# A two-layer trunk in split fp32 on one core: another deal of the first chunk's taps, six products moved behind the convolution's output, and two weights whose low parts VectorE subtracts

## The chip, the cores and the metric

The kernel runs on one core of one Trainium2 chip. The metric is device time in microseconds (us) of one execution. The kernel before was timed three times: 1772.48, 1773.45 and 1774.38 us, median 1773.45 us. Its profiled execution took 1771.89 us by the same clock, of which the trace covers a span of 1770.1 us; so the profiled execution is 1.56 us faster than the median, and 1.79 us of it lie outside the span.

The engines are called as in the profile: PE is TensorE's matmul, PEld its weight load, DVE is VectorE, ACT is ScalarE, POOL is GpSimd, SP is SyncE, which here only issues DMAs.

## What is computed

Two residual layers over a sequence of 1024 positions with 1024 channels, one sequence, everything in fp32. Each sub-layer is an RMS norm, a shift and scale from a conditioning vector, the sub-layer, a gate and the residual sum. Layer 0 mixes tokens with a convolution module, layer 1 with a pooling mixer; both have a gated feed-forward part of width 2816.

```python
def conformer_conv(h, w1, b1, w_dw, b_dw, ln_g, ln_b, w2, b2):
    u = h @ w1 + b1
    a, g = jnp.split(u, 2, axis=-1)
    u = a * jax.nn.sigmoid(g)
    u = depthwise_causal_conv(u, w_dw) + b_dw        # width 31
    u = jax.nn.silu(layer_norm(u, ln_g, ln_b))       # over channels
    return u @ w2 + b2

for i in range(2):
    sh_m, sc_m, g_m, sh_f, sc_f, g_f = split(silu(c) @ ada_w[i] + ada_b[i])
    h = modulate(rms_norm(x, norm_mix_g[i]), sh_m, sc_m)
    y = conformer_conv(h, ...) if i == 0 else multiscale_pool(h, ...)
    x = x + (1 + g_m) * y
    h = modulate(rms_norm(x, norm_ffn_g[i]), sh_f, sc_f)
    x = x + (1 + g_f) * ((silu(h @ w_gate[i]) * (h @ w_up[i])) @ w_down[i])
return rms_norm(x, final_g)
```

## The kernel before

**Tiles.** Channels lie on the 128 partitions, in 8 tiles (KT = 8); the sequence is cut into two chunks of 512 positions, A and B. Every fp32 operand of a product is kept as a high part and a low part. A weight tile of 128 x 1024 so becomes a pair of `w` tiles, and for each of its 8 pieces k PE makes three products of 512 columns (`products`): high weight by high activation, high weight by low activation, low weight by high activation. Twenty-four products make one output tile.

**Lows of weights.** `load_weight` brings the raw weight with an SP DMA, ACT casts it to the high part, and the low part is raw minus high. In most cases it is made without DVE: ACT writes minus the high part into the low tile, and POOL issues a DMA that adds the raw weight on top of it from memory (line 461, seen in the profile as `POOL L461 DMA w<-in_...`). Weights that are wrapped in `Own` are instead subtracted by DVE (`w<-raw,w`). There are nine `w` buffers and four `raw` buffers.

**The depthwise convolution.** 31 taps for each of 8 channel tiles and each chunk. For tile 7 of chunk A, PE does it. For the others, `Taps.step` deals each tap to DVE or to POOL. On DVE a tap is one instruction (`ca<-u,taps,ca`). On POOL it is two: ACT scales the row (`ny<-u,taps` in chunk A, `pr<-u,taps` in chunk B) and POOL adds it to a running sum (`pa<-pa,ny` or `pa<-pa,pr`). At the end DVE adds POOL's sum to its own (`ca<-pa,ca`) and puts the last tap in place (`u<-u,taps,ca`).

**What sets the order.** PE's instructions run in the order in which the code emits them, written out by hand. The other engines' order is made from the same program by a scheduler that respects dependences. Which engine gets a tap or a part of a side task is decided while the program is written out, by estimated clocks: `clock["PE"]` moves with every product, `clock["V"]` (DVE) and `clock["G"]` (POOL) with every instruction by the prices in `PRICES`, and `pace` hands out work to whichever engine's clock is not more than `AHEAD` in front of PE's. A `Task` is a chain that says at each stop how long it must be left alone; the stops are looked up in `LOAD`. The stop "mean" stands in `layer_norm_silu` for chunk A between the last sum of channels (`acc<-acc,u`) and PE's `mean` product; the larger the number, the later on PE's clock the mean is written out.

**The stretch that matters.** In order of PE: products `a` and `g` of chunk B with A's taps running on DVE and POOL beside them; the layer norm of A (`mean`, then `var`, then `rstd`) placed among those products; then the last pair of B, emitted by `conv_split`: all of its `a`, then the first `EARLY_K` pieces of its `g`, the rest being held back (`st["split"]`). Then `y`, the second matrix of the convolution for A, 8 output tiles. Then the first feed-forward norm of A. `norm_split` puts the held products of `g` around its two steps on PE: `COVER_K` says up to which piece k they go ahead of `var` and ahead of `rstd`, the rest follows `rstd`; `COVER` says how many idle products (`idle<-ones`, results thrown away) are added at each of the three places. With the norm's results (`hhi`, `hlo`) the feed-forward part of A starts: `ffn_first` runs gate and up of f = 0 and gate of f = 1 together, then up of f = 1; `ffn_p1` runs gate and up of the following f; after every two f the group `dn` multiplies by the down weights. In this stretch DVE and POOL do B's taps. `fa` is the list of these units; its first three are replaced by `ffn_first` and the unit of f = 2 with its weights wrapped in `Own`. The fourth is the first `dn` group, which needs `dn` weights of f = 0 and 1.

**Names in the profile.** Every DVE, ACT and POOL computation has the line 119 (`Engine.issue`), every product the line 142; so instructions are told apart by the tiles they write and read.

Of the kernel before, what the change touches and what calls it, by code (L numbers as in the profile page):

```python
# [45 lines left out]
PHTAPS = 29  # L46
PHLEN = 135
OUT_B = 3
LOAD = {"load": 9.0, "late": 5.0, "second": 11.0, "settle": 8.0, "mean": 11.0, "slow": 18.0, "next": 4.0}
AHEAD = 4  # L50
STRETCH = 1.35
LATER = 300
WARM = (22, 10, 6)
COVER, EARLY_K, COVER_K = (2, 2, 4), 3, (5, 8)
FREE = 4
EARLY_X = 4
WARM_LAST = 5
# [67 lines left out]
def trunk(ctx, tc, xT, c, vec, ada, adan, w1, w2, wgu, wdn, wpl, wph, out):  # L125
# [488 lines left out]
    def own(unit_):  # L614
        return unit_[0], tuple(Own(w) for w in unit_[1])
# [109 lines left out]
    class Taps:  # L725
# [10 lines left out]
        def step(self, e):  # L736
            ch, p = self.ch, self.p
            n = ch.n
            u = st["u", ch.i, p]
            w = lambda j: wdw[:, j * KT + p : j * KT + p + 1]  # L740
            if self.done:
                return False
            if self.next < CW - 1:
                if e == "V" and self.acc is None and sum(isinstance(t, Taps) and t.acc is not None for t in tasks) >= 2:
                    return False
                if e == "G":
                    if self.acc is None and self.part is None and sum(isinstance(t, Taps) and t.part is not None for t in tasks) >= 2:
                        return False
                    if self.next >= CW - 3:
                        return False  # L750
                j = self.next
                self.next += 1
                if e == "V":
                    src = u[:, j : j + n]
                    if self.acc is None:
                        self.acc = spare_bank("ca")
                        V_.tensor_scalar(self.acc, src, w(j), V("conv_bdw", p), op0=MUL, op1=ADD)
                    else:
                        V_.scalar_tensor_tensor(self.acc, src, w(j), self.acc, op0=MUL, op1=ADD)
                    st["tap"] = V_.last.ins.name  # L760
                    twin = [t for t in tasks if isinstance(t, Taps)][:2]
                    if len(twin) == 2 and twin[0] is self:
                        i, k = (tasks.index(t) for t in twin)
                        tasks[i], tasks[k] = tasks[k], tasks[i]
                elif self.part is None:
                    self.part = window(n, "pa")
                    G_.tensor_scalar(self.part, u[:, j : j + n], w(j), 0.0, op0=MUL, op1=ADD)
                    if st.get("behind norm"):
                        tc.add_manual_dep(G_.last.ins, st.pop("behind norm"), synced, reason="behind the norm")
                else:  # L770
                    pr = temp(n, "ny", 2) if ch.i == 0 else temp(n, "pr")
                    S_.activation(pr, u[:, j : j + n], AF.Copy, scale=w(j))
                    scaled_taps.append(S_.last.ins)
                    G_.tensor_tensor(self.part, self.part, pr, op=ADD)
                return True
            if e != "V":
                return False
            if self.part is not None:
                V_.tensor_tensor(self.acc, self.part, self.acc, op=ADD)
            d = u[:, HALO : HALO + n]  # L780
            V_.scalar_tensor_tensor(d, d, w(CW - 1), self.acc, op0=MUL, op1=ADD)
            self.done = True
            tasks.remove(self)
            left = st["taps", ch.i]
            left[p] = True
            return True
# [271 lines left out]
    def ffn_first(ch, l, between):  # L1058

        def emit(take):  # L1060
            h = st["h", ch.i]
            outs = [output(name, False) for name in ("gate", "up", "gate")]
            wts = [take() for _ in outs]
            for k in range(KT):
                for o, wt in zip(outs, wts):
                    products(o, wt, k, h[k], k == 0, k == KT - 1)
                pace()
                if k == 3:
                    between()
                if k == FREE:  # L1070
                    del scaled_taps[:]
            gated(ch, 0, outs[:2], held=scaled_taps)
            hold[0] = st["silu"]
            wt = take()
            outs.append(output("up", False))
            for k in range(KT):
                products(outs[3], wt, k, h[k], k == 0, k == KT - 1)
                if k % 4 == 3:
                    pace()
                    if k == 3:  # L1080
                        del scaled_taps[:]
            gated(ch, 1, outs[2:], held=scaled_taps)
        return emit, tuple(wgu[l, f, i] for f in range(2) for i in range(2))
# [980 lines left out]
    taps(B, *range(KT))  # L2064
    put("ln_b", lambda: layer_norm_silu(B))
    fa = ffn(A, 0, False)
    fa[:GROUP + 1] = [ffn_first(A, 0, gates_on), own(fa[GROUP])]
    for i, (e, ws) in enumerate(fa):
        if i == len(fa) - OUT_B:
            need("ln_b")  # L2070
# [182 lines left out]
```

## Time and profile before

| what | value |
|---|---|
| median of three timed runs | 1773.45 us |
| profiled execution, own time | 1771.89 us |
| span of its trace | 1770.1 us |
| PE busy in the span | 1738.5 us |
| DVE busy | 1374.0 us |
| ACT busy | 987.1 us |
| POOL busy | 564.0 us |

A line of the timeline gives the start in us, the time that the instructions took, engine, line, operation, output and inputs by the program's names, shapes and how many were merged; in brackets stands the idle time of the engine just before it and who ended it. A line of the chain of work gives start, duration, engine, name and the number of instructions. A line of a table of windows gives the stretch, its length, then for PE, PEld, DVE, ACT and POOL the busy time with the number of instructions, then the granted PE clock as a share of full speed, the DMA share and GB/s. A line of the DMA view ends with the size of one transfer and the median time from its issue to its landing. Waits are listed as "who waited, for what: us in total, times, longest".

### The profile page before, as it was taken

The page shows a single profiled execution, that of the slowest core. Times are in us where ns is not written, and L with a number is a line of the kernel's source. Part 1 is how long each engine was busy: PE and PEld are TensorE (multiplying, and loading weights), DVE is VectorE, ACT ScalarE, POOL GpSimd, SP SyncE. Part 2 cuts the span into 40 slices and gives each one's busy share as a digit, 9 for nine tenths or more (in the row PEclk, how much of TensorE's full clock was granted, in tenths as well). Part 3 has the DMA queues.
Part 4 walks back from the last instruction along what each step waited for, and adds up shares of the span by engine and source line. Part 5 has one row for each costly group of instructions (what it writes and reads, how often), then busy time and mean ns, then how long its engine had stood idle before and what let it go on. Part 6 is the DMA issues. An engine that isn't in the chain of part 4 may idle for free.

```text
span 1770.1 us, 24916 instructions
## 1 busy us (share of the span) xinstructions
PE 1738.5 (98%) x8830; PEld 1460.3 (82%) x8830; DVE 1374.0 (78%) x2273; ACT 987.1 (56%) x1566; POOL 564.0 (32%) x607
## 2 busy tenths in 40 slices
PE   9999999999999999999999999999999999999997
PEld 7777787788888888899999888887888888877996
DVE  7999657788775327989996977976888788777885
ACT  4776656767656455555555356464444444444653
POOL 0599614887834121211102713411011111111112
PEclk9999999999999999999999999999999999999999
DMA  9959746988988988877675477798778888887551
GB/s 296 305 171 251 196 118 157 243 214 213 240 204 205 240 218 195 222 210 215 198 213 132 123 179 177 166 235 272 226 216 262 240 242 223 252 251 201 155 150 54
DMA packets 145151, 366.26 MB, mean 207 GB/s; under 512 B 14977, under 2 KB 32641, under 8 KB 145026
## 3 DMA queue, kind: packets, MB, share of 16 engines
q1 hardware_dynamic: 109600, 265.56, 44.5%
q0 software_dynamic: 34272, 98.06, 31.3%
q8 instruction: 69, 1.13, 0.3%
q10 hardware_dynamic: 1154, 1.05, 0.2%
q14 instruction: 56, 0.46, 0.1%
HBM read 340.50 MB, written 24.12 MB: 206 GB/s over the span
## 4 chain that ended last, share of the span: by engine, by line
PE 89%; DMA 4%; issue 2%; DVE 2%; ACT 1%; POOL 1%; SPq 0%; DVEq 0%; POOLq 0%; ACTq 0%
PE gate L142 24%; PE dn L142 24%; PE up L142 23%; PE y L142 6%; PE a L142 3%; PE g L142 3%; PE first L142 2%; DMA adaw<-in_adan_dram 1%; DMA t<-t 1%; DMA w<-in_wdn_dram 1%; PE ada L142 1%; DMA front<-front 1%; DVE x L119 1%; ACT w L119 0%; DMA w<-in_wgu_dram 0%
## 5 line engine op out<-in xcount | busy, mean ns | idle before, releaser
L119 ACT CAST w<-raw 128x1024 fp32r<-128x1024 f32 (+1 forms) x314 | 262.7, 838 | 110.6 <-PE up L142 46.1
L142 PE MATMUL dn<-ghi,w 128*128 128x512 f32 (+1 forms) x944 | 302.6, 386 | 2.7 <-DMA w<-in_wdn_dram 2.1
L142 PE MATMUL gate<-hhi,w 128*128 128x512 f32 (+1 forms) x968 | 295.1, 373 | 1.3 <-ACT hhi L119 0.8
L142 PE MATMUL up<-hhi,w 128*128 128x512 f32 (+1 forms) x968 | 294.6, 372 | 0.0
L119 ACT ACTIVATE w<-raw 128x1024 fp32r<-128x1024 f32 (+1 forms) x182 | 172.9, 950 | 193.1 <-PE up L142 60.0
L119 DVE SCALAR_TENSOR_TENSOR x<-dn,gains,x 128x512 f32<-128x512 f32 (+1 forms) x312 | 225.5, 733 | 46.9 <-PE dn L142 45.2
L142 PEld LDWEIGHTS gate<-hhi,w 128*128 128x128 f32 x968 | 178.1, 189 | 34.6 <-ACT hhi L119 1.0
L142 PEld LDWEIGHTS dn<-ghi,w 128*128 128x128 f32 x944 | 176.3, 189 | 36.6 <-DMA w<-in_wdn_dram 2.5
L142 PEld LDWEIGHTS up<-hhi,w 128*128 128x128 f32 x968 | 178.0, 188 | 31.8
L142 PE MATMUL dn<-glo,w 128*128 128x512 f32 (+1 forms) x472 | 181.9, 385 | 0.1
L142 PE MATMUL gate<-hlo,w 128*128 128x512 f32 (+1 forms) x484 | 180.2, 372 | 0.3 <-DVE hlo L119 0.3
L142 PE MATMUL up<-hlo,w 128*128 128x512 f32 (+1 forms) x484 | 179.8, 372 | 0.0
L119 DVE SCALAR_TENSOR_TENSOR ca<-u,taps,ca 128x512 f32<-128x512 f32 x251 | 174.9, 747 | 0.9
L461 POOL DMA_DIRECT2D w<-in_wgu_dram x76 | 69.0, 907 | 247.3 <-ACT w L119 233.2
L1547 POOL DMA_DIRECT2D x<-scaled x48 | 41.6, 868 | 325.9 <-ACT scaled L119 170.2
L119 DVE TENSOR_TENSOR w<-raw,w 128x512 fp32r<-128x512 f32 (+1 forms) x132 | 108.9, 831 | 41.8 <-ACT w L119 34.9
L119 POOL TENSOR_TENSOR pa<-pa,pr 128x512 f32<-128x512 f32 x92 | 131.5, 1509 | 8.4 <-ACT pr L119 6.4
L119 DVE TENSOR_TENSOR t<-t,up 128x512 f32<-128x512 f32 (+1 forms) x76 | 49.4, 650 | 89.7 <-PE up L142 87.1
L1215 POOL DMA_DIRECT2D w<-in_wgu_dram x42 | 37.1, 891 | 256.3 <-ACT w L119 109.5
L119 POOL TENSOR_TENSOR pa<-pa,ny 128x512 f32<-128x512 f32 x77 | 104.0, 1381 | 8.5 <-ACT ny L119 5.8
L142 PEld LDWEIGHTS gate<-hlo,w 128*128 128x128 f32 x484 | 91.3, 189 | 16.6 <-DVE hlo L119 0.6
L142 PEld LDWEIGHTS up<-hlo,w 128*128 128x128 f32 x484 | 91.1, 188 | 15.9
(292 smaller groups left out, 3844.4 us busy)
## 6 DMA issues: line engine op xcount, KB each, us to landing
raw<-in_wgu_dram SPq DMA_DIRECT2D x148, 512.0 KB, 5.6
t<-t SPq DMA_DIRECT2D x224, 256.0 KB, 5.2
w<-in_wgu_dram POOLq DMA_DIRECT2D x76, 512.0 KB, 8.2
adaw<-in_ada_dram SPq DMA_DIRECT2D x64, 512.0 KB, 5.1
raw<-in_wdn_dram SPq DMA_DIRECT2D x62, 512.0 KB, 5.5
raw<-in_w_dram SPq DMA_DIRECT2D x42, 512.0 KB, 6.2
w<-in_wdn_dram POOLq DMA_DIRECT2D x34, 512.0 KB, 8.3
adaw<-in_adan_dram SPq DMA_DIRECT2D x32, 512.0 KB, 5.7
```

The costliest lines, as they stand in the source:

```text
L119: self.last = self.order(getattr(self.eng, name)(out, *args, **kw))
L142: last_mm[0] = nc.tensor.matmul(out, lhsT, rhs, start=start, stop=stop, **kw).ins.name
L461: order(nc.gpsimd.dma_start(as_src(lo), src, accum_op=ADD))
L1215: order(nc.gpsimd.dma_start(lo, src, accum_op=ADD))
L1547: order(nc.gpsimd.dma_start(st["kept", "x"][at], t, accum_op=ADD))
```

## The change

Three edits, in four places of the text.

First, chunk A's taps: each POOL sum of chunk A now moves POOL's estimated clock by a further 0.08, and the stop "mean" is 7 in place of 11. Second, the products held for the norm: `EARLY_K` is 1 in place of 3, so 3 products of the last `g` and not 9 stand ahead of `y`; `COVER_K` (4, 7) puts 9 ahead of `var`, 9 ahead of `rstd` and 3 behind it, in place of 6, 9 and none; the idle products of the three places are 0, 0 and 2 in place of 2, 2 and 4. Third, the down weights of f = 0 and f = 1 are wrapped in `Own`, so DVE subtracts their lows.

```diff
-LOAD = {"load": 9.0, "late": 5.0, "second": 11.0, "settle": 8.0, "mean": 11.0, "slow": 18.0, "next": 4.0}
+LOAD = {"load": 9.0, "late": 5.0, "second": 11.0, "settle": 8.0, "mean": 7.0, "slow": 18.0, "next": 4.0}
 AHEAD = 4
+SLOWER = 0.08
...
-COVER, EARLY_K, COVER_K = (2, 2, 4), 3, (5, 8)
+COVER, EARLY_K, COVER_K = (0, 0, 2), 1, (4, 7)
...
                     S_.activation(pr, u[:, j : j + n], AF.Copy, scale=w(j))
                     scaled_taps.append(S_.last.ins)
                     G_.tensor_tensor(self.part, self.part, pr, op=ADD)
+                    if ch.i == 0:
+                        clock["G"] += SLOWER
...
-    fa[:GROUP + 1] = [ffn_first(A, 0, gates_on), own(fa[GROUP])]
+    fa[:GROUP + 2] = [ffn_first(A, 0, gates_on), own(fa[GROUP]), own(fa[GROUP + 1])]
```

Where this moves instructions is shown at three places; a number in a name is that of one tile, and the numbers differ between the two programs for the same tile.

POOL, ahead of chunk A's mean: `pa` is POOL's running sum of the last channel tile, `ny` a row that ACT scaled, `DMA w` the issue of a weight's low, and `u<-u,ny` is the first work behind the mean. Before:

```order
L461 DMA w_1966<-in_w_dram 128x1024
L119 TENSOR_TENSOR pa_1728<-pa_1728,ny_1849 128x512
L119 TENSOR_TENSOR pa_1728<-pa_1728,ny_1881 128x512
L119 TENSOR_TENSOR pa_1728<-pa_1728,ny_1885 128x512
L119 TENSOR_TENSOR pa_1728<-pa_1728,ny_1889 128x512
L461 DMA w_2086<-in_w_dram 128x1024
L119 TENSOR_TENSOR pa_1728<-pa_1728,ny_1907 128x512
L119 TENSOR_TENSOR pa_1728<-pa_1728,ny_1911 128x512
L461 DMA w_2097<-in_w_dram 128x1024
L119 TENSOR_TENSOR u_653<-u_653,ny_2037 128x512
```

With the change:

```order
L462 DMA w_1957<-in_w_dram 128x1024
L120 TENSOR_TENSOR pa_1756<-pa_1756,ny_1914 128x512
L120 TENSOR_TENSOR pa_1756<-pa_1756,ny_1918 128x512
L462 DMA w_2080<-in_w_dram 128x1024
L462 DMA w_2091<-in_w_dram 128x1024
L120 TENSOR_TENSOR u_653<-u_653,ny_2031 128x512
```

Two sums in place of six stand behind the same weight's DMA, and none behind the next one. Over the whole of chunk A POOL has 74 sums in place of 77, DVE 129 taps in place of 126; for chunk B POOL has 96 in place of 92 and DVE 136 in place of 140. The `mean` product stands at the same place of PE's order as before.

PE, from the end of `y` to the first gate product: `g` are the held products, `idle` the idle ones. Before:

```order
L142 MATMUL ada_2522<-adaw_2533,ccols 32x256 x4
...
L142 MATMUL g_2184<-hhi_767,w_2097 128x512
L142 MATMUL idle_2646<-ones 128x128 x2
L142 MATMUL var_2627<-ones,acc_2368 128x1 x4
L142 MATMUL g_2184<-hhi_769,w_2096 128x512
...
L142 MATMUL g_2184<-hhi_773,w_2097 128x512
L142 MATMUL idle_2662<-ones 128x128 x2
L142 MATMUL rstd_2678<-ident,col_2666 128x128 x4
L142 MATMUL idle_2683<-ones 128x128 x4
L142 MATMUL gate_2738<-hhi_2611,w_2517 128x512
```

With the change:

```order
L143 MATMUL ada_2510<-adaw_2521,ccols 32x256 x4
...
L143 MATMUL g_2178<-hhi_765,w_2091 128x512
L143 MATMUL var_2615<-ones,acc_2356 128x1 x4
L143 MATMUL g_2178<-hhi_767,w_2090 128x512
...
L143 MATMUL g_2178<-hhi_771,w_2091 128x512
L143 MATMUL rstd_2663<-ident,col_2651 128x128 x4
L143 MATMUL g_2178<-hhi_773,w_2090 128x512
L143 MATMUL g_2178<-hlo_774,w_2090 128x512
L143 MATMUL g_2178<-hhi_773,w_2091 128x512
L143 MATMUL idle_2671<-ones 128x128 x2
L143 MATMUL gate_2724<-hhi_2599,w_2505 128x512
```

The last piece of `g` now stands behind `rstd`, and six more products than before lie between `y` and the gate. On ACT nothing changes place here: the last weight instruction ahead of the norm's first `hhi` writes a low tile into a buffer that PE must have released (`w_2723` before, `w_2709` now).

DVE, between the subtractions of f = 2 (the first row of each piece is the second of these) and the first `dn` products: `ny<-ny,up` is the gated product of f = 1, `mod<-adac` a column sum that waits for PE. Before:

```order
L119 TENSOR_TENSOR w_2926<-raw_2923,w_2925 128x1024
L119 SCALAR_TENSOR_TENSOR ca_2814<-u_1831,taps,ca_2814 128x512
L119 TENSOR_TENSOR ny_2912<-ny_2912,up_2874 128x512
L119 SCALAR_TENSOR_TENSOR ca_2786<-u_1627,taps,ca_2786 128x512
...
L119 TENSOR_TENSOR mod<-adac_3048,vecs 128x8
```

With the change:

```order
L120 TENSOR_TENSOR w_2912<-raw_2909,w_2911 128x1024
L120 SCALAR_TENSOR_TENSOR ca_2800<-u_1816,taps,ca_2800 128x512
L120 TENSOR_TENSOR w_2928<-raw_2925,w_2927 128x1024
L120 TENSOR_TENSOR ny_2898<-ny_2898,up_2860 128x512
L120 SCALAR_TENSOR_TENSOR ca_2772<-u_1615,taps,ca_2772 128x512
L120 TENSOR_TENSOR w_2936<-raw_2933,w_2935 128x1024
...
L120 TENSOR_TENSOR mod<-adac_3032,vecs 128x8
```

Two subtractions are new on DVE, one ahead of and one behind the gated product of f = 1; the two `DMA w<-in_wdn_dram` of these weights are gone from POOL, and ACT's two instructions that wrote minus the high part with them.

## The prediction

> **What bounds the kernel now.** I read the page's busy line first, then the chain of work that ended last, then PE's waits, and only then the timelines around each wait that the change touches.
>
> ```profile
> PE 1738.5 (98%) x8830; PEld 1460.3 (82%) x8830; DVE 1374.0 (78%) x2273; ACT 987.1 (56%) x1566; POOL 564.0 (32%) x607
> PE 89%; DMA 4%; issue 2%; DVE 2%; ACT 1%; POOL 1%; SPq 0%; DVEq 0%; POOLq 0%; ACTq 0%
> PE dn L142 <- DMA w<-in_wdn_dram: 5.8, 3, 3.1
> PE mean L142 <- DVE acc L119: 3.0, 1, 3.0
> PE gate L142 <- ACT hhi L119: 0.8, 1, 0.8
> PE gate L142 <- DMA w<-in_wgu_dram: 0.5, 1, 0.5
> 322.66 11.62 PE dn L142 x43
> 356.03 10.88 PE dn L142 x48
> ```
>
> PE is busy for 98% and carries 89% of the chain. So only three things can move the end: fewer products, shorter waits of PE, a higher clock of PE. The products stay, but for 12 idle ones of 128 columns each. The four waits quoted are those beside which the change stands; of the 5.8 of `dn` one, of 2.09, belongs to it. The last two lines, of the chain, give the price of a product: 10.88 / 48 = 0.227 us. By it 43 products take 9.75 us; the first `dn` group took 11.62 for 43. So 1.87 us were lost there behind the wait itself.
>
> **Part 1, the mean of chunk A.** The timelines of PE, DVE, POOL and ACT around it:
>
> ```profile
> 201.58 0.39 PE L142 MATMUL g<-hhi,w 128*128 128x512 f32 x1
> 204.94 1.10 PE L142 MATMUL mean<-acc,ones 128*128 128x512 f32 x2 [2.98 <-DVE acc L119]
> 192.60 2.33 DVE L119 SCALAR_TENSOR_TENSOR ca<-u,taps,ca 128x512 f32<-128x512 f32 x3
> 194.84 0.74 DVE L119 SCALAR_TENSOR_TENSOR u<-a,vecs,t 128x512 f32<-128x512 f32 x1
> 201.80 0.70 DVE L119 TENSOR_TENSOR ca<-pa,ca 128x512 f32<-128x512 f32 x1 [6.21 <-POOL pa L119]
> 203.38 1.42 DVE L119 TENSOR_TENSOR acc<-acc,u 128x512 f32<-128x512 f32 x2
> 192.21 5.73 POOL L119 TENSOR_TENSOR pa<-pa,ny 128x512 f32<-128x512 f32 x4 [1.71 <-ACT ny L119]
> 199.12 2.65 POOL L119 TENSOR_TENSOR pa<-pa,ny 128x512 f32<-128x512 f32 x2 [0.37 <-ACT ny L119]
> ```
>
> PE waits 2.98 us for DVE's sum `acc`, but DVE itself had nothing to do for 6.21 us: POOL's last sum, ending at 201.77, is the bound. From there DVE needs until 203.38 + 1.42 = 204.80, so 3.0 us. PE would have been there at 204.94 - 2.98 = 201.96.
>
> With the change only two sums follow the weight's DMA ahead of the four quoted first, so POOL ends about 192.21 + 5.73 / 2 = 195.1. DVE has three taps more: (194.84 - 192.60) / 3 = 0.75 each, so its own work ends at 195.58 + 2.24 = 197.8 in place of 195.58. DVE is then the later one, and `acc` is ready at 197.8 + 3.0 = 200.8, 1.1 us ahead of PE. The earlier "mean" stop moves nothing on PE, since the product stands at the same place of its order. The wait goes: **-2.98 us**. The bounds: nothing is gained if POOL's last sums still come behind 201.8, and no more than the wait can go. I take the whole, since the two sums' rows lie nearest. Late next is the norm's `var`:
>
> ```profile
> 214.37 1.41 DVE L119 TENSOR_TENSOR acc<-acc,t 128x512 f32<-128x512 f32 x2
> 217.98 0.95 PE L142 MATMUL var<-ones,acc 128*128 128x1 f32 x8
> ```
>
> It stands 13.0 us behind the mean in PE's order, and its sum of squares was ready at 215.8, 2.2 us ahead. On ACT the copy of the mean now meets a weight cast that used to run in the wait, at up to 1.0 us, and one more pair of weight instructions, 2.1 us, goes ahead of the last square; DVE's `u<-a` of 0.75 goes from ahead of the sum's end to behind it. That is 1.4 to 2.4 us against 2.2, and I cost it at nothing; if the cover is gone it costs 0.2.
>
> **Part 2, six products behind y.** Six of nine products of `g` ahead of `y` go, and come back at the norm, where two idle groups and half of a third are taken out.
>
> ```profile
> 227.29 0.39 PE L142 MATMUL y<-vhi,w 128*128 128x512 f32 x1
> 219.42 0.87 POOL L461 DMA_DIRECT2D w<-in_w_dram  x1 [3.52 <-ACT w L119]
> w<-in_w_dram POOLq DMA_DIRECT2D x2, 512.0 KB, 7.7
> 278.77 1.06 ACT L119 ACTIVATE w<-raw 128x1024 fp32r<-128x1024 f32 x1 [1.00 <-PE g L142]
> 279.33 1.13 PE L142 MATMUL rstd<-ident,col 128*128 128x128 f32 x8
> 282.13 0.50 PE L142 MATMUL gate<-hhi,w 128*128 128x512 f32 x1 [0.78 <-ACT hhi L119]
> 277.23 0.86 POOL L461 DMA_DIRECT2D w<-in_wgu_dram  x1 [7.81 <-ACT w L119]
> 285.32 0.73 PE L142 MATMUL gate<-hhi,w 128*128 128x512 f32 x2 [0.52 <-DMA w<-in_wgu_dram]
> ```
>
> The norm is a chain of latencies from the end of `y` to the gate, through all engines, in which PE's own products only fill gaps. What starts `y` earlier by 6 x 0.227 = 1.36 us so brings the gate earlier by as much, and the six products fit the gaps: ahead of `var` three take the place of an idle group, ahead of `rstd` nine stay and the chain through DVE is longer than they are, behind it three stand where idle products did.
>
> Two things take part of it back. First, the second weight of `y`: its low is the transfer issued by POOL at 219.42; 7.7 to 8.0 us later it lands at 227.1 to 227.4, on the clock of before. It is needed five products after `y` begins, which is now 227.29 - 1.36 + 5 x 0.227 = 227.06. So PE stands for 0.0 to 0.4 us; I take 0.3, as the two landings behind that median differ. Second, ACT. The instruction at 278.77 waits until PE releases a buffer of the held weight; its release now comes behind `rstd`, with the second of the last three products: in the same frame at about 279.33 + 1.13 + 2 x 0.227 = 280.9, so with its 1.06 it ends at 282.0. Behind it in ACT's queue stand all the `hhi`. The first of them, some 0.7 long, was done for the gate at 282.13, so it began at 281.4; it and the gate come 0.6 us later than the shift says. But the third product of the next weight waits for the transfer issued at 277.23, until 285.32, and that one hangs on the end of `y` alone and not on this ACT instruction. The 0.6 are taken out of its 0.52 of waiting, and 0.1 is left. So part 2 gives 1.36 - 0.3 - 0.1, about **-1.0 us**; the ends are 0 (low late by the whole shift) and -1.36.
>
> **Part 3, the lows of the first dn weights.**
>
> ```profile
> 319.18 0.48 PE L142 MATMUL dn<-ghi,w 128*128 128x512 f32 x1
> 322.66 0.99 PE L142 MATMUL dn<-ghi,w 128*128 128x512 f32 x2 [2.09 <-DMA w<-in_wdn_dram]
> 313.66 1.20 POOL L461 DMA_DIRECT2D w<-in_wdn_dram  x1
> 226.00 1.22 DVE L119 TENSOR_TENSOR w<-raw,w 128x1024 fp32r<-128x1024 f32 x1
> 305.92 2.27 DVE L119 TENSOR_TENSOR w<-raw,w 128x1024 fp32r<-128x1024 f32 x1
> 307.20 1.03 ACT L119 CAST w<-raw 128x1024 fp32r<-128x1024 f32 x1
> 319.36 0.17 DVE L119 TENSOR_TENSOR mod<-adac,vecs 128x8 f32<-128x8 f32 x1 [3.32 <-PE adac L142]
> ```
>
> The low of the second `dn` weight was issued by POOL at 313.66, behind its tap sums, and landed 9.0 us later; PE stood 2.09 us. A subtraction on DVE takes 1.22 us alone (226.00) and 2.27 beside POOL's sums (305.92). ACT has cast the second weight by 308.2. On DVE the first subtraction starts behind the tap that follows 305.92, at 308.8, and with the gated product (0.7), a tap (0.7) and the second subtraction between, all are done by 308.8 + 2 x 2.27 + 1.4 = 314.7. The second low is needed five products after 319.18, at 320.3. So the wait goes: -2.09. Behind the two new instructions on DVE wait the gated product of f = 1 and then taps; the former comes 2.3 us later, and its low half has until 319.7. DVE's 4.5 us more are covered by 3.32 us of idle at 319.36 and by later waits for PE. If that cover is gone, they cost at most what a late gated product costs, some 1 us.
>
> Then the clock. The table of windows:
>
> ```profile
> 204.94:207.00 2.06, 2.06 (x19) 0.72 (x19) 0.25 (x1) 0.58 (x1) 0.19 (x1) 1.00 0.72 201
> 322.60:324.60 2.00, 1.94 (x5) 1.59 (x6) 1.34 (x2) 0.82 (x3) 2.00 (x4) 0.59 1.07 295
> 326.40:330.00 3.60, 3.60 (x17) 3.00 (x16) 2.66 (x5) 1.52 (x3) 3.60 (x4) 1.00 1.05 249
> ```
>
> Right behind the wait of `dn` the granted clock was 0.59, and 1.00 again from 326.4 on. That is the 1.87 us above. Without the wait I expect no fall, so part 3 gives 2.09 + 1.87, **-3.96 us**; its ends are -2.09 (the fall stays) and -3.96. Behind the mean's wait, longer by 0.9, the clock stayed at 1.00, so what a wait does to the clock is not certain.
>
> The Trainium skill ("TensorE: Matmul & The Clock Gate", "Part 1: The HAM clock gate") says that the clock goes to half after at least one idle window of about 3.4 us, in windows that run free of the program. By that neither wait would have been long enough, and the sum below would lose the 1.87 us; the rows at 322.60 speak against it, those behind the mean for it.
>
> **What comes late next.** POOL's work behind `dn`, and the end of chunk B's taps:
>
> ```profile
> 334.87 0.89 POOL L461 DMA_DIRECT2D w<-in_wgu_dram  x1 [2.95 <-ACT w L119]
> 345.44 0.62 PE L142 MATMUL gate<-hhi,w 128*128 128x512 f32 x2
> 509.07 1.41 DVE L119 TENSOR_TENSOR acc<-acc,u 128x512 f32<-128x512 f32 x2
> 520.43 1.02 PE L142 MATMUL mean<-acc,ones 128*128 128x512 f32 x2
> ```
>
> The low of the gate of f = 4 was issued at 334.87 and, at some 8.4 us (between the 7.7 and the 9.0 above), landed at 343.3 for a product at 345.44: 2.1 us to spare. PE comes 3.96 us earlier behind `dn`, ACT's buffer release with it, but POOL's sums don't all. POOL had 2.95 us of idle before it. So between 0 and 1.9 us can be lost; I take 0.1. For chunk B, `acc` was ready at 510.5 and PE came at 520.4. PE now comes 7.8 earlier, at 512.6. DVE has two subtractions more (4.5) and three more low halves of 0.7, four taps fewer (-3.0), so about +3.6, but starts its taps 4 us earlier: no wait, with 2 us to spare.
>
> **The sum.** -2.98 - 1.0 - 3.96 + 0.1 = -7.8 us. From the profiled 1771.89 that is 1764.1; against the median of 1773.45, which I take as the level to compare with, **1765.6 us**.
>
> **The rivals.**
> - *The mean still waits.* DVE's three taps and its adds end behind 202, or POOL's last sums wait for ACT behind the cast. Against: 1.1 us of room. For: the whole room is an estimate. With half of the wait left, -7.8 + 1.5 = -6.3: 1767.1; with all, 1768.6.
> - *The gain of y is eaten*, by the low of its second weight, or by ACT's queue ahead of `hhi`: +1.0, 1766.6.
> - *The clock still falls*, at `dn` for a reason other than the wait, or for a new stop of some 1 us at the gate of f = 4, or in the norm, where PE now stands with less to cover it. It costs 1.87, with the stop itself 2.8: 1767.5 to 1768.4. For the fall at `dn` alone I give 0.05, for the other two 0.08. That the wait has no part in the fall is what the clock-gate page of the Trainium skill, as told above, would make of it.
> - *The change does less than it says:* the price on POOL and the shorter stop cancel each other. The order excludes it for the sums ahead of the mean; for the time it is the first rival.
> - *Slower: chunk B's taps end late.* Place: the mean of B. POOL has four sums more, DVE 3.6 us more. If `acc` is ready at t behind 512.6, PE stands for t - 512.6. From t = 520.4, 9.9 us later than before, all is given back, and a measurement tells it as slower from 523.9; at 525 the time is 1778. Only 3.6 of these are in the rows; the rest would have to be DVE work held up beside POOL, at up to 1.05 us for each two-input subtraction. I see no six of them.
>
> **How the numbers follow.** Forecast 0.56; the mean still waits 0.10; y's gain eaten 0.10; the clock falls 0.13 (0.05 and 0.08); two or three of these at once, which leaves 3 us or less, 0.07; slower 0.04. A difference of 0.2%, 3.5 us, is about what can be told from none; so it counts as faster below 1769.9: 0.89 (the first four), same 0.07, slower 0.04. The range goes from 1763.7 (all of part 2, 0.4; all of the gate's 0.5 of waiting; and the quickest of the three runs in place of the median, 1.0) to 1769.0, which takes in each single rival but the last.
>
> **What would show it.** In the changed profile: no wait of `mean` for `acc`, and DVE idle before `ca<-pa,ca` for less than 1 us; `y` 4.0 to 4.4 us earlier, with a stop of up to 0.4 at its fifth product; no wait of the first `dn` group and a clock of 1.00 in it, so 10.9 us for 48 products; no new wait at the gates of f = 3 to 5, and none at B's mean. I am wrong if the clock falls at another place, or if DVE, with 129 taps, is the one for which the mean waits.

## The result

The changed kernel's median was 1762.05 us (1759.81 to 1764.37, 6 runs) against 1772.97 us of the kernel before (6 runs). The ratio is 0.9939, 95% interval 0.9926 to 0.9952, or 10.8 us faster, 8.5 to 13.1. A second set of runs gave 0.9947 (0.9935 to 0.9959): 9.4 us, 7.3 to 11.5. The forecast was 7.8 us, with a range that ended at 9.8. It is faster, as forecast; the gain is 1.6 to 3.0 us larger, and the first median lies 1.65 us below the lower end of the range, 1763.7.

The profiled execution of the changed kernel took 1762.23 us (span 1760.5). The lines of its page that answer to those shown of before:

```profile
PE 1732.3 (98%) x8818; PEld 1455.0 (83%) x8818; DVE 1379.9 (78%) x2277; ACT 987.2 (56%) x1565; POOL 562.0 (32%) x603
PE 88%; DMA 4%; POOL 3%; issue 2%; DVE 2%; ACT 1%; SPq 0%; DVEq 0%; POOLq 0%; ACTq 0%
```

And of PE's waits:

```profile
PE dn L143 <- DMA w<-in_wdn_dram: 3.8, 2, 2.9
PE gate L143 <- DMA w<-in_wgu_dram: 1.2, 1, 1.2
PE gate L143 <- ACT hhi L120: 1.1, 1, 1.1
```

The wait of the mean is no longer in the list, and of the waits of `dn` the first one, of 2.09, is gone; the two left stand in layer 1. New is one of 1.2 at a gate. The timelines at the four places, first the mean on PE, DVE and POOL:

```profile
201.26 1.02 PE L143 MATMUL mean<-acc,ones 128*128 128x512 f32 x2
196.67 0.69 DVE L120 TENSOR_TENSOR ca<-pa,ca 128x512 f32<-128x512 f32 x1
198.59 1.42 DVE L120 TENSOR_TENSOR acc<-acc,u 128x512 f32<-128x512 f32 x2
191.25 2.96 POOL L120 TENSOR_TENSOR pa<-pa,ny 128x512 f32<-128x512 f32 x2 [1.16 <-ACT ny L120]
```

POOL's last sum ends at 194.2, DVE doesn't wait for it any more, and `acc` is ready at 200.0, 1.3 us ahead of PE (forecast 1.1). Then `y`, the first gate and the first `dn` group, and DVE's last subtraction for it:

```profile
222.17 0.39 PE L143 MATMUL y<-vhi,w 128*128 128x512 f32 x1
277.66 0.50 PE L143 MATMUL gate<-hhi,w 128*128 128x512 f32 x1 [1.08 <-ACT hhi L120]
315.13 0.62 PE L143 MATMUL dn<-ghi,w 128*128 128x512 f32 x2
306.96 2.31 DVE L120 TENSOR_TENSOR w<-raw,w 128x1024 fp32r<-128x1024 f32 x1
```

The table of windows for the beginning of that group:

```profile
313.50:317.00 3.50, 3.50 (x19) 2.95 (x19) 0.55 (x2) 2.44 (x4) 3.50 (x4) 1.00 0.92 341
```

The gate waits 0.3 longer for `hhi`, the ACT queue that was forecast, and as forecast it costs nothing behind it. The low is there 5.9 us before the second weight's third product, at 315.1 or so; PE doesn't stop, and its clock (the third number from the end of the window's line) is 1.00. Last, the gate of f = 4, in POOL's and PE's timelines:

```profile
321.86 8.13 POOL L120 TENSOR_TENSOR pa<-pa,pr 128x512 f32<-128x512 f32 x6
329.58 1.26 POOL L462 DMA_DIRECT2D w<-in_wgu_dram  x1
337.56 0.73 PE L143 MATMUL gate<-hhi,w 128*128 128x512 f32 x2 [1.19 <-DMA w<-in_wgu_dram]
```

POOL issues this low behind six tap sums in a row, and PE stops 1.19 us for it.

To compare many kernels, the profiles are cut into stages by the starts of PE's instructions. N goes from `var` of chunk B's first norm (73.58 in before) to its `rstd`; M from `pz` (188.28) to the second group of `ada` products, which stands behind the mean; Y from there to `y` (227.29); D from the second `up` of `ffn_first` (286.35) to the gate of f = 3 (334.11); G from there to B's mean (520.43); L, in layer 1, from a `rstd` at 1162.76 to an `up` product at 1234.18. The table is worked out from the timelines of one profile each, in us. In the expectations below, W, D, P and L are also names of theories; in my own text these letters are the stages, unless the word theory stands before them. Theory L is that stage L is shorter because of the first edit.

| profile | N | M | Y | D | G | L |
|---|---|---|---|---|---|---|
| before | 7.18 | 17.69 | 21.32 | 47.76 | 186.32 | 71.42 |
| before, again | 7.46 | 18.02 | 22.46 | 48.66 | 186.33 | 71.34 |
| held products alone | 7.47 | 19.43 | 21.88 | 49.75 | 186.32 | 70.88 |
| dn lows alone | 7.41 | 18.00 | 22.78 | 43.81 | 186.61 | 71.71 |
| taps undone | 7.19 | 17.77 | 21.58 | 43.80 | 187.23 | 69.05 |
| mean filled | 7.18 | 17.85 | 21.58 | 46.20 | 186.32 | 71.43 |
| mean filled, dn lows | 7.16 | 18.44 | 21.58 | 43.82 | 186.83 | 70.56 |
| stop alone | 7.20 | 22.70 | 21.37 | 46.32 | 186.32 | 73.03 |
| price alone | 6.74 | 17.12 | 21.20 | 47.94 | 186.32 | 71.16 |
| taps alone | 6.34 | 15.03 | 21.32 | 45.58 | 186.32 | 69.83 |
| held undone | 6.34 | 14.36 | 21.32 | 43.80 | 186.35 | 69.91 |
| dn undone | 6.34 | 15.14 | 19.96 | 50.35 | 186.32 | 69.56 |
| after | 6.34 | 15.18 | 19.96 | 43.78 | 187.81 | 69.63 |
| after, again | 6.34 | 14.66 | 19.96 | 43.81 | 187.73 | 68.99 |

Undisturbed, Y is 21.32 with nine products ahead of `y` and 19.96 with three. In the row "price alone" the mean stands behind the second `ada`, so there only M and Y together, 38.32, can be set against the other rows.

### The profile page after: what moved, and what is told of

Same layout as the page of the kernel before. It is cut to its first block, busy times and chain, and to the rows that moved or that the text cites. A ratio compares the mean times of both kernels' runs of the same rounds, so it can differ in the third digit from the quotient of the medians.

```text
span 1760.5 us, 24895 instructions
## 1 busy us (share of the span) xinstructions
PE 1732.3 (98%) x8818; PEld 1455.0 (83%) x8818; DVE 1379.9 (78%) x2277; ACT 987.2 (56%) x1565; POOL 562.0 (32%) x603
## 4 chain that ended last, share of the span: by engine, by line
PE 88%; DMA 4%; POOL 3%; issue 2%; DVE 2%; ACT 1%; SPq 0%; DVEq 0%; POOLq 0%; ACTq 0%
PE gate L143 24%; PE dn L143 24%; PE up L143 23%; PE y L143 6%; PE a L143 3%; PE g L143 3%; PE first L143 2%; POOL pa L120 2%; DMA adaw<-in_adan_dram 1%; DMA t<-t 1%; PE ada L143 1%; PE var L143 1%; PE rstd L143 1%; DMA front<-front 1%; DVE x L120 0%
## 5 line engine op out<-in xcount | busy, mean ns | idle before, releaser
L120 DVE TENSOR_TENSOR w<-raw,w 128x512 fp32r<-128x512 f32 (+1 forms) x134 | 113.2, 851 | 39.6 <-ACT w L120 34.1
L120 POOL TENSOR_TENSOR pa<-pa,pr 128x512 f32<-128x512 f32 x96 | 137.9, 1501 | 8.9 <-ACT pr L120 7.1
```

The lines of the kernel that those rows point to most:

```text
L120: self.last = self.order(getattr(self.eng, name)(out, *args, **kw))
```

## The experiments

All ratios are to the kernel before on the same chip; the microseconds are the ratio times 1771.

**The kernel before, once more** (no edit).

> The kernel before once more, for the clock of each of its executions. In the profile of before PE's clock fell to half after the wait at the first dn group (one stretch of 3.41 us) and at a dn wait of layer 1 at 1214 us (6.83 us), but not after the longer wait at the mean (205 us); all falls begin at whole multiples of 3.413 us from each other. Theory W (windows): the clock is judged in windows that run free of the program, so the mean's wait of 2.98 us takes it down in most executions, and the profiled one was a lucky one: the executions differ in mean clock (0.992 to 0.997), the slower the lower, and a new profile has a fall behind the mean in 3 of 4 cases. Theory D (downstream): the falls are fixed by the program, every execution has those of the profile (0.994), and the 3 us of unforeseen gain come from later stages.

Ratio 1.0000 (0.9992 to 1.0009), 1767.6 to 1775.4 us. This time the clock fell behind the mean. PE's timeline, and the table of windows:

```profile
204.56 1.55 PE L142 MATMUL mean<-acc,ones 128*128 128x512 f32 x2 [2.98 <-DVE acc L119]
```

```profile
204.90:208.30 3.40, 3.40 (x19) 0.99 (x18) 1.47 (x3) 1.34 (x3) 1.42 (x2) 0.53 0.80 172
```

The wait is the same 2.98 to the hundredth, but the clock is 0.53 behind it, where the profile of before had 1.00. M and Y are together 1.5 us longer. So the program alone doesn't fix where the clock falls; what the traces show of it is in the last section.

**The first edit alone.**

```diff
-LOAD = {... "mean": 11.0, ...}
+LOAD = {... "mean": 7.0, ...}
...
+SLOWER = 0.08
...
+                    if ch.i == 0:
+                        clock["G"] += SLOWER
```

> Only the first edit: POOL's sums of chunk A priced higher, the stop at the mean at 7. W: the wait of 2.98 goes and with it the falls that it causes in most executions, 1.7 to 3.4 us each: 4.5 to 5.5 us faster than before in the median. D: 3.0 faster, and whatever is more shows in the profile as shorter waits behind 1200 us.

0.9965 (0.9953 to 0.9976): 6.2 us faster, 4.3 to 8.3. Three microseconds, the price of the wait, lie outside the interval. The table shows a second place: N, at 80 us, is 6.34 and not 7.18 to 7.47.

**The third edit alone.**

```diff
-    fa[:GROUP + 1] = [ffn_first(A, 0, gates_on), own(fa[GROUP])]
+    fa[:GROUP + 2] = [ffn_first(A, 0, gates_on), own(fa[GROUP]), own(fa[GROUP + 1])]
```

> Only the third edit: the first dn weights' lows subtracted by DVE. In the changed kernel's profile that group was 3.98 us shorter, but the gate of f = 4 stopped for 1.2 us. W: the fall there comes only in part of the executions (the wait of 2.09 is little more than half of a window), so 2.1 to 3.9 less 1.2 to 1.5: 0.8 to 2.7 faster. D: 3.96 less 1.2: 2.8 faster.

0.9979 (0.9969 to 0.9988): 3.7 us faster, 2.1 to 5.5; the values of both theories lie in the interval. D falls by 4.0 against the profile of before, and G grows by 0.3 only: without the other edits the new stop at the gate of f = 4 isn't there.

**The mean's wait filled with idle products.** PE is busy while it waits, and the mean is as late as before.

```diff
         b = bank("mean")
+        if ch.i == 0:
+            for _ in range(11):
+                matmul(b[:, :P], ones, ones, start=True, stop=True)
         matmul(b, ones, acc, start=True, stop=True)
```

> The kernel before, but with 11 idle products of 128 columns (2.9 us of PE, result overwritten) right ahead of the mean product of chunk A: the mean comes as late as before, PE only isn't idle while it waits. W: the falls behind the mean go, 1.5 to 2.5 us faster in the median, and no fall within 10 us behind the mean in the profile. D: no change (within 0.5 us).

0.9991 (0.9981 to 1.0001): 1.6 us faster, from 3.4 faster to 0.2 slower. The table of windows right behind the mean:

```profile
203.20:206.60 3.40, 3.40 (x24) 1.84 (x25) 1.57 (x3) 1.80 (x4) 1.52 (x2) 1.00 0.78 188
```

No fall, though the idle products made M and Y 0.4 longer. The value is what theory W said, but the interval takes in zero, and the clocks of the executions don't bear it out. The mean granted clock is on record for every execution: it averages 0.9931 over these 11 and 0.9934 over the 28 of the kernel before beside them. One stretch of 3.41 us at half clock less in each execution would have made it 0.001 higher. So this run doesn't show that the filling made falls rarer.

**The changed kernel again, and each edit undone.**

Of the last three of these four, each is the changed kernel with the diff of one edit reversed.

> The changed kernel once more, beside the next three and on their chip. In six profiles so far the clock fell 15 times, each time at the end of a window of 3.41 us on one fixed grid in which PE had stood for 1.99 us or more, and never after one with 1.72 or less. W: averaged over the grid's place, the sum of the parts is the mean 2.98 + 0.8 falls of 1.2, the norm 1.5, the dn group 2.1 to 2.9 + half a fall, less 1.2 to 1.5 at the gate of f = 4: 7 to 9 us faster than before. D: 10 to 11 us faster, as in the first six executions, with the part over 8 behind 1200 us.

0.9947 (0.9935 to 0.9959): 9.4 us faster, between the two theories, whose values both touch the interval of 7.3 to 11.5.

> The changed kernel without its first edit. W: the mean waits again for 2.98 and the clock falls there in 4 executions of 5: 3.5 to 4.5 slower than the changed kernel. D: 3 slower. If the first edit also acts on the dn group (in its run alone that wait was 1.49 in place of 2.09 to 2.89), nothing of that is seen here, since DVE makes these lows.

0.9984 (0.9972 to 0.9996): 2.8 us faster than before where the whole change gives 9.4. So the first edit is worth some 6.6 here, as alone. Both theories said 3 to 4.5; as the difference of two values that are each good to some 2 us, the 6.6 alone doesn't exclude that.

> The changed kernel without its second edit: nine products ahead of y, idle products at the norm. Both theories: 1.4 to 1.6 us slower than the changed kernel, y 1.36 later against the mean, no other wait changed.

0.9951 (0.9938 to 0.9964), 8.7 us faster than before: this kernel and the changed one can't be told apart. Y is 1.36 longer, but G is 186.35 and not 187.8. In the profiles, what the second edit gains at `y`, the stop at the gate of f = 4 takes back.

> The changed kernel without its third edit. In the profiles the dn group costs 43.8 to 45.6 us from the third up product to the gate of f = 3 where the first edit stands alone (wait 1.49, no fall), 46.2 to 48.7 where it doesn't. If the first edit takes half of the dn wait by itself, undoing the third costs only 0 to 2 us: 1.8 for the wait and, without the 1.2 to 1.5 at the gate of f = 4, some 0.5 in sum. If the two are independent, it costs 4 less 1.4: 2.6 slower than the changed kernel.

0.9973 (0.9961 to 0.9985): 4.8 us faster than before, so the third edit is worth 4.6 in place. PE's timeline at the dn group:

```profile
314.50 0.73 PE L143 MATMUL dn<-ghi,w 128*128 128x512 f32 x2 [0.86 <-DMA w<-in_wdn_dram]
318.32 1.22 PE L143 MATMUL dn<-ghi,w 128*128 128x512 f32 x2 [2.85 <-DMA w<-in_wdn_dram]
```

Both weights' lows are now late, 3.7 us in place of 2.09. They come behind POOL's tap sums: PE begins the group 6.2 us earlier than in before, the second low lands only 4.3 us earlier. By this profile the first edit doesn't take half of the wait by itself, which was the first alternative; the 2.6 of the other lies within what the two intervals allow.

**The second edit alone.**

```diff
-COVER, EARLY_K, COVER_K = (2, 2, 4), 3, (5, 8)
+COVER, EARLY_K, COVER_K = (0, 0, 2), 1, (4, 7)
```

> Only the second edit. The norm itself: y 1.36 earlier against the mean. But the dn lows are POOL's and come at a time that PE doesn't set (undoing the third edit in the changed kernel gave that group 50.4 us in place of 43.8), so the dn wait grows by what the norm gains: 0 to 1 us faster than before. If the parts are independent: 1.4 faster. The dn wait 1212 us: 71 us for the stage from 1163 to 1234 us if that stage hangs on the first edit (theory L), 68 to 73 if it is chance.

1.0010 (1.0000 to 1.0020): 1.8 us slower, 0 to 3.5. PE's timeline at the dn group, and the chain of work there:

```profile
326.25 1.22 PE L142 MATMUL dn<-ghi,w 128*128 128x512 f32 x2 [2.86 <-DMA w<-in_wdn_dram]
```

```profile
326.25 9.82 PE dn L142 x31
```

The wait grew from 2.09 to 2.86, and 31 products took 9.82 in place of 7.0: the clock fell for two windows. D is 49.75, 2.0 more than in the profile of before, so in this profile the 1.36 are more than spent there.

**The price and the stop apart.**

> Only the price on POOL's sums, the stop at the mean left at 11: chunk A's deal is that of the changed kernel, but the mean stands 14 products later in PE's order. Theory P: the whole gain of the first edit comes from the deal, both at the mean (2.98 and the fall behind it) and at the first norm of chunk B at 80 us, where PE waited 0.7 to 1.0 for DVE without the edit and not with it. Then this is 5 to 6 faster than before, as the whole first edit. Rival: the norm at 80 us hangs on the stop; then the wait there is as before and 1 us of it is missing.

0.9985 (0.9974 to 0.9995): 2.7 us faster, 0.9 to 4.6, so less than the 5 to 6 of theory P. With the mean behind 12 more products `a` and a group of `ada` PE waits elsewhere, for the norm behind it (PE's timeline):

```profile
221.98 1.16 PE L143 MATMUL rstd<-ident,col 128*128 128x128 f32 x8 [1.22 <-DVE col L120]
```

> Only the stop at the mean at 7, the price left out: the deal is that of before and the mean stands 12 products earlier in PE's order. P: DVE's sum is ready at the same time, so PE waits 2.98 + 12 x 0.227 = 5.7 us, which holds a whole window: the clock falls always; 2.7 to 4 us slower than before. The rival: the norm at 80 us gains 0.95 and it is 2 to 3 slower.

1.0020 (1.0009 to 1.0030): 3.5 us slower. The wait is 5.64, as worked out, and M 5.0 longer:

```profile
203.17 2.05 PE L142 MATMUL mean<-acc,ones 128*128 128x512 f32 x2 [5.64 <-DVE acc L119]
```

So each half needs the other: the price frees the sum earlier, the stop keeps the mean where it was. N is 7.20 here and 6.74 with the price: that gain goes with the deal.

**Against the stop at the gate of f = 4.** Four more kernels have DVE subtract more lows, or price POOL's sums in both chunks.

```diff
-    fa[:GROUP + 2] = [ffn_first(A, 0, gates_on), own(fa[GROUP]), own(fa[GROUP + 1])]
+    fa[:GROUP + 4] = [ffn_first(A, 0, gates_on), own(fa[GROUP]), own(fa[GROUP + 1]), fa[GROUP + 2], (fa[GROUP + 3][0], (Own(fa[GROUP + 3][1][0]), *fa[GROUP + 3][1][1:]))]
```

> The changed kernel, and in addition the low of the gate of f = 4 subtracted by DVE. The stop there, 1.19 in the changed kernel's profile, goes: 1.2 to 1.5 us faster than the changed kernel, if DVE's subtraction, which waits for ACT's cast and a free buffer, doesn't hold up the taps or dn's sums behind it; if it does, the stop stands at the gate of f = 4 or at the next dn group as before and the time is the same.

0.9947 (0.9935 to 0.9958), as the changed kernel. The stop went on to the next dn group:

```profile
347.80 0.73 PE L143 MATMUL dn<-ghi,w 128*128 128x512 f32 x2 [0.62 <-DMA w<-in_wdn_dram]
```

The next has also that group's lows on DVE (`own(fa[GROUP + 4])` as one more entry of the list):

> The changed kernel, and DVE also subtracts the lows of the gate of f = 4 and of the dn weights of f = 2 and 3. With the gate of f = 4 alone the stop only moved to that dn group (0.6, and the stage was 0.5 shorter than in the changed kernel). If POOL's queue is what makes these lows late, the stage from the gate of f = 3 to chunk B's mean falls to 186.3 from 187.7: 1.0 to 1.5 faster than the changed kernel. If DVE then becomes late, a wait of PE for DVE shows in that stage or at B's mean, and the time is the same or slower.

0.9949 (0.9932 to 0.9965). G is 187.68, but chunk B's mean stands six products later in its PE order (1.36), so 186.32 of it compare, and PE has no wait over 0.25 us in it. The stop is gone; the 1.5 us can't be seen in the time, whose interval is 6 us wide. It is not shown to beat the changed kernel.

```diff
-    fa[:GROUP + 2] = [ffn_first(A, 0, gates_on), own(fa[GROUP]), own(fa[GROUP + 1])]
+    fa[:GROUP + 3] = [ffn_first(A, 0, gates_on), own(fa[GROUP]), own(fa[GROUP + 1]), own(fa[GROUP + 2])]
```

> The changed kernel, and DVE also subtracts the lows of gate and up of f = 3, so POOL issues two transfers less ahead of that of the gate of f = 4. If POOL's queue is what makes that one late, the stop there goes (1.49 in two profiles) and nothing comes in its place: 1.0 to 1.5 faster than the changed kernel. Rival: DVE, with two subtractions more, makes dn's group or the gate late, and the stage is 187.7 as before. The stage from 1163 to 1234 us: about 69.7 by L, 68 to 73 if it is chance.

0.9962 (0.9949 to 0.9976), slower than the changed kernel by 2.7, with intervals that overlap. The stop is 2.68. POOL issues that transfer behind 25 sums of chunk B in place of 24, and 0.9 us later than in the changed kernel, while PE comes 0.7 us earlier:

```profile
338.31 0.74 PE L143 MATMUL gate<-hhi,w 128*128 128x512 f32 x2 [2.68 <-DMA w<-in_wgu_dram]
330.52 0.89 POOL L462 DMA_DIRECT2D w<-in_wgu_dram  x1
```

```diff
-                    if ch.i == 0:
-                        clock["G"] += SLOWER
+                    clock["G"] += SLOWER
```

> The changed kernel with the price on POOL's sums in both chunks: 93 sums of POOL for chunk B in place of 96. If POOL's queue makes the low of the gate of f = 4 late by its tap sums, the stop of 1.2 shrinks or goes: 0.5 to 1.5 faster. Rival: three sums fewer over the whole chunk don't change those ahead of that transfer, and the time is the same. The stage from 1163 to 1234 us as in the run before.

0.9975 (0.9965 to 0.9984), 4.4 us faster than before. PE doesn't stop for the transfer, but only because it comes later: it has stopped 3.09 for DVE at the gate of f = 3 (PE, DVE and POOL). Here too 25 sums stand ahead of that transfer, so what fewer sums ahead of it would do was not tried:

```profile
327.74 0.50 PE L143 MATMUL gate<-hhi,w 128*128 128x512 f32 x1 [3.09 <-DVE x L120]
322.30 4.72 DVE L120 TENSOR_TENSOR glo<-t,ghi 128x512 fp32r<-128x512 f32 x1
319.64 6.83 POOL L120 TENSOR_TENSOR pa<-pa,pr 128x512 f32<-128x512 f32 x5
```

**Idle products in the mean's wait, and the third edit** (both diffs above).

> The kernel before with idle products in the mean's wait and with the third edit: no fall of the clock in layer 0, but the mean as late as before and chunk A's deal as before. Against the third edit alone (3.7 faster than before) it lacks only the falls behind the mean: 4.5 to 5.5 faster than before by W, 3.7 if the falls there are of no weight. The stage from 1163 to 1234 us: about 71.3 by L, since chunk A's deal is that of before; 68 to 73 if it is chance.

0.9975 (0.9966 to 0.9985): 4.4 us faster than before, 2.7 to 6.0, against 3.7 of the third edit alone. The two values can't be told apart, so this doesn't decide whether the falls behind the mean have weight.

## Why the prediction was wrong in its size

**Part 1 is the step that failed**, in its words "no more than the wait can go". The wait went as forecast, by the mechanism that was named: POOL's last sums, then DVE with 1.3 us to spare. But the edit is worth 6.2 us (4.3 to 8.3) alone and some 6.6 in place, not 2.98. So a wait of 2.98 was not the most that could go with it. The profiles show two more things in it:

- *Falls of the clock behind the mean.* I took the granted clock of one execution, 1.00 behind the mean's wait, for a property of the program. Of the five profiles with the wait of 2.98 unfilled, four have a fall there; the one I had was the fifth. By Y, against 21.32 or 19.96, a fall cost 1.14 (before again), 1.46 (dn lows alone), 1.62 (taps undone) and 1.92 (held products alone, two windows); M took 0.1 to 1.7 more. Spread over the five, Y gives 1.2 us and M 0.5 that this edit saves besides the wait. Over all executions the granted clock averages 0.9942 (5) with the first edit alone against 0.9934 (28), so at 0.001 for a stretch some 0.8 stretches of half clock fewer, give or take 0.4. The filled wait, as said, doesn't confirm it.
- *Chunk B's first norm*, at 80 us, which I left out, because none of the lines of waits that I quoted pointed there. N is 7.16 to 7.47 in the eight profiles without the price, 6.34 to 6.40 in nine with the whole first edit and 6.74 with the price alone: 0.8 to 1.1 us. The timelines of PE, DVE and POOL in before, and then in the changed kernel:

```profile
80.76 1.16 PE L142 MATMUL rstd<-ident,col 128*128 128x128 f32 x8 [0.20 <-DVE col L119]
76.69 1.64 POOL L119 TENSOR_TENSOR pa<-pa,ny 128x512 f32<-128x512 f32 x1
76.15 2.21 DVE L119 TENSOR_SCALAR col<-col 128x4 int32<-128x4 int32 x1
219.37 0.17 DVE L119 TENSOR_SCALAR col<-col 128x4 int32<-128x4 int32 x1
```

```profile
79.39 1.05 PE L143 MATMUL rstd<-ident,col 128*128 128x128 f32 x8
74.77 1.81 POOL L120 TENSOR_TENSOR pa<-pa,ny 128x512 f32<-128x512 f32 x1
75.62 1.00 DVE L120 TENSOR_SCALAR col<-col 128x4 int32<-128x4 int32 x1
```

The DVE instruction is a step of the norm's chain, at whose end PE's `rstd` waits. It takes 0.17 at 219 us, where POOL has no sums, and 2.21 beside them; with the new deal POOL's sums stand otherwise and it takes 1.00. Both times it ends within 0.04 us of the end of the POOL sum that is shown (78.36 and 78.33; 76.62 and 76.58). It takes 2.21 to 2.51 in the eight profiles without the price and 0.98 to 1.30 in the ten with it, and `rstd` waits for DVE in all of the eight (0.20 to 0.96) and in none of the ten. Part of this gain is lost on a later wait for `ada` weights, 0.71 at 84 us in the changed kernel in place of 0.49, and 0.77 at 192 us.

The wait, these 0.8 to 1.1 and the 1.7 of the falls make 5.5 to 5.8, which lies in the interval of 4.3 to 8.3.

**Part 2** was right in the norm: `y` 1.36 earlier in Y, with no stop at its second weight (I had put 0.3). As a gain of the kernel, 1.0, it wasn't found: alone the edit is 1.8 us slower (0 to 3.5), in place it is nothing that can be told. By the profiles its 1.36 come back as waits for POOL's transfers, at `dn` where those lows are POOL's, at the gate of f = 4 otherwise.

**Part 3**: -3.96 forecast, -3.98 in D of the profiled pair; in time 3.7 alone and some 4.6 in place. That the pair agrees to 0.02 is luck: the fall at this wait, 1.87 of the 3.96, comes in some executions only. In "mean filled" and "stop alone" the wait is 2.11 and 2.21, no fall follows, and D is 46.20 and 46.32, 2.4 to 2.5 above the profiles with the third edit and not 4. The rival for that group, a fall for a reason other than the wait, didn't come: no profile with the third edit has a fall in it. By the Trainium skill ("TensorE: Matmul & The Clock Gate", "Part 1: The HAM clock gate") a wait of 2 us should do nothing; the rows go against that.

**What comes late next**: the low of the gate of f = 4 was costed at 0.1, with 1.9 as the end; it took 1.49 and 1.41 in G. This stop was named in a rival, together with a fall of the clock; the stop came, and no fall followed it. I counted PE's arrival and POOL's idle time, and not that two more sums came ahead of the transfer in POOL's queue: 24 sums of chunk B stand ahead of it in the changed kernel, 22 in before.

**The slower rival** (chunk B's taps late) didn't come: there is no wait at B's mean.

**The sum.** For the profiled pair, by the table and the starts at the norm: M -2.51, N -0.84, Y -1.36, the norm behind it -0.1, D -3.98, G +1.49, L -1.79, all else -0.5: -9.6, the difference of the spans. Against the average of before comes the fall behind the mean, over 1 us. Over the executions the whole change raises the mean granted clock from 0.9935 (15) to 0.9958 (6), some 2.4 stretches of half clock, where the sum of the prediction had one.

**What stays open** is L, 1.8 us in that pair. It is 70.6 to 73.0 in seven of the eight profiles without the price and 69.05 in the other; 69.0 to 69.9 in the five with the whole first edit in the table; but 71.16 with the price alone, and 71.35, 67.57, 69.56 and 70.59 in the four that go against the stop. No engine's order differs in that stage between before and the changed kernel. The table of windows for it, before and then after:

```profile
1162.76:1234.18 71.42, 67.58 (x286) 54.50 (x284) 58.49 (x93) 41.80 (x71) 9.28 (x9) 0.95 0.85 244
```

```profile
1155.29:1224.92 69.63, 64.96 (x286) 52.38 (x284) 58.48 (x93) 41.88 (x71) 9.30 (x9) 1.00 0.89 252
```

PE runs the same products. In before it is busy 2.62 us longer, at a clock of 0.95 and not 1.00, and stands 0.83 us less. So the 1.8 of this pair is a fall of the clock (two stretches, at 1213.83), less some waiting. All eighteen profiles part in this way: PE is busy for 64.8 to 65.5 us in the five without a fall in this stage, 65.8 to 66.9 in the ten with one stretch, and 67.1 to 68.2 in the three with two. What is left open is whether the first edit makes these falls rarer: eight profiles without the price have ten stretches there, nine with the whole edit have five, too few to tell it from chance.

## What to carry to other kernels

In these traces a wait of the tensor engine cost more than its length when it filled over half of a clock window, and one profile doesn't tell: count the chance of a fall, not the fall that you see. Where a wait ends on something that the waiting engine doesn't set, such as a transfer that another engine issues behind its own queue, time gained ahead of it can be lost there; the three edits were worth some 10 us together, and the second one alone gained nothing. Here an edit made for one wait also gained 1 us at a place 120 us ahead of it: go through every stage in which the deal of work changes. Undo each part of a change as well as making it alone.

## What the runs showed of the hardware

**The clock's windows.** By the trace's record of the granted clock, it fell 41 times in the eighteen profiles between 30 us and the tail (from 1740 us on), always to half and for one or two stretches of 3.41 us. Within a profile all falls begin on one grid of 3.4133 us: in before at 322.95, 1213.83 and 1599.53 us, so 261 and 113 steps apart. From profile to profile the grid stands elsewhere against the program. Of the 41 falls, 39 began at the end of a window of that grid in which PE had been idle for 1.90 us or more; the other two had 1.70 and 1.42. Every window with 1.90 us or more was followed by half clock, and twenty with 1.37 to 1.86 were not; between 1.4 and 1.9 the idle time alone doesn't tell. A second stretch followed in eleven falls: in these PE stood for 0.64 us or more within the first stretch, in the other thirty for 0.53 or less. In before the mean's 2.98 were cut by the grid into 1.52 and 1.46: no fall. At `dn` all 2.09 lay in one window: a fall. The Trainium skill ("TensorE: Matmul & The Clock Gate", "Part 1: The HAM clock gate") states the length and that the windows run free, and the traces agree; it asks for a whole idle window, and here a little over half of one was enough.

**POOL's sums hold up DVE for longer than one of them.** In the kernel with the price in both chunks, `glo<-t,ghi`, 0.7 us behind 570 us, where POOL has no tap sums, took 4.72 and ended 0.55 us behind the last of five sums that POOL ran back to back, in 6.83 us. The Trainium skill ("SBUF — State Buffer", "Who interferes with whom") says that a DVE instruction with two inputs in SBUF contends with a GpSimd instruction that reads SBUF, for a shared port pair that is locked. The trace agrees that DVE stands beside POOL's sums, and it stood through three or more of them in a row.
